# One layer of a hybrid encoder: norm weights as rows, first weights in eight pieces, row sums earlier, last gate projections by quarters

## The chip, the cores and the metric

The kernel runs on one core of a Trainium2 chip. The metric is the device time of one execution in microseconds (us), given as the median of several runs. An engine works through its own queue in order: PE is the matrix engine (PEld its weight loads), DVE the vector engine, ACT the scalar engine, POOL the general engine, SP the engine that issues the DMAs. Each waits on semaphores for what another has made.

## The reference

x has 2048 rows of 1024 columns (f32). The layer normalises each row, multiplies by one input matrix of 1024 x 3344 columns, and splits the result between two head groups.

```
h = rms_norm(x, norm_w)
proj = h @ w_in      # dn_q, dn_k, dn_v, dn_z, beta, decay | sw_q, sw_k, sw_v, sw_z
dn = gated_deltanet_bidir(...)          # 4 heads of 128: conv of 5 taps on q, k, v, SiLU, l2 norm,
                                        # gated delta rule in chunks, forward and backward
dn = rms_norm(dn, dn_out_norm_w) * silu(dn_z)
sw = windowed_gqa_with_sinks(...) * silu(sw_z)   # 8 query and 2 kv heads of 64, window 128
out = x + concat(dn, sw) @ w_out
```

Inputs, results and sums are f32.

## The kernel before

The kernel keeps f32 accuracy with the faster f32r matmuls: each operand is split into a rounded part `hi` (ACT, `AF.Copy`) and the rest `lo` (DVE, subtract), and a product is three matmuls, hi x hi, hi x lo, lo x hi.

**Phase A** (`phase_a`) goes through the rows in two halves of 1024; a half is two blocks of 512 rows, and a block four chunks of 128. A block of normalised, transposed rows is a pair of tiles `xhi[b]`, `xlo[b]`; the pool holds two such pairs, so the second half's blocks 2 and 3 take the places of 0 and 1.

- `xprep_rows` (L102) makes block 0: for each chunk it loads 128 rows of x (`xr`, L104 and L115), sums the squares on ACT (L119), makes the factor on POOL (L120, L121), multiplies by factor and norm weights (`nwb`, one DMA that reads the 1024 weights for each of the 128 partitions, L110) on DVE (L122), transposes on PE (L126) and splits (L129, L130).
- `xprep` (L132) makes blocks 1, 2 and 3: it loads the four row chunks (L137), sums the squares (L138), makes the factors (L139, L140), spreads them over a PSUM bank `rb` with PE (L143), loads x transposed (`xt`, L150), scales it on DVE (L153) and splits (L154, L155).
- `load_w` (L159) loads a weight matrix in four pieces of two row groups each (`ws`) and splits them (L165, L166). The split weights have two places, `wh`/`wl`.
- `proj_seq` (L181) projects a chunk of rows for keys, values, queries and the small gates (`pq_kv`, 272 columns, and `pq_q`, 256): 24 matmuls per chunk. `proj_feat` (L171) projects 128 features of a block (`pf_z`, `pf_c`, 512 columns): 24 matmuls.
- `gate_pair` (L192) takes two groups of gate features through both blocks of a half (tanh on ACT L199, multiply on DVE L200), and stores 1024 columns of each (L202). `conv_pair` (L204) does the same for two groups of q, k or v with the convolution on DVE (L224).
- `attend` (L314) does the window attention of a chunk: scores `s` (L326, L327), mask and maximum on DVE (L328), exponential on ACT (L333), division on POOL (L342), transposes on PE (L347), split (L351, L352) and products `po` (L354, L355).

Tiles of 1024 columns (`xr`, `xt`, gate results, convolution tiles) come from one pool, `bp`, with four places in a ring; the banks of `pq`, `pf` and `rb` from one, `pj`, with three.

The main loop (L369 to L401) makes a half's blocks, its keys, values and queries, then attends chunk after chunk, and after each takes one or two of ten entries of a list `fill`: two gate pairs for the attention, six convolution pairs, and the two gate pairs 12 and 14 for the delta net, which come last in a half. `xprep(2)` stands at the head of the second half.

**Phase B** (`phase_b`) takes the four delta-net heads one after another. `pre_front` (L586) makes the chunk matrices, `pre_back` (L665) solves the triangular systems (31 steps on DVE, L681 and L685, then PE), `scan` (L724) carries the state through 16 steps from both ends, and `post` (L783) normalises four chunks and multiplies by the gate: squares on ACT (L790), a power of four columns on POOL (L793), scaling (L795), transposes. The output projection follows (`out_sw`, `out_dn`, L526).

**The order.** `set_order` (L843) plans the order of all five queues by itself. It lists what each instruction needs (data, and for a tile the end of the last use of the tile whose place it takes), gives each a price (`cost`, L971), plans forward and backward several times and fixes the best order by added dependencies. A change of the program can thus move any instruction on its queue.

Of the kernel before, what the change touches and what calls it, by code (L numbers as in the profile page):

```python
# [7 lines left out]
F32 = mybir.dt.float32  # L8
F32R = mybir.dt.float32r
AF = mybir.ActivationFunctionType  # L10
ALU = mybir.AluOpType
# [4 lines left out]
P = 128  # L16
S = 2048
D = 1024
KC = 8
NCH = 16  # L20
HC = 8
WC = 272
# [41 lines left out]
def phase_a(ctx, tc, t, ident, nw, bd, gp, mix_sw, kq_d, v_d, zdn_d, zsw_d, q_pool):  # L64
# [37 lines left out]
    def xprep_rows(b):  # L102
# [7 lines left out]
        dma(nwb, t["nw"].partition_broadcast(P))  # L110
# [21 lines left out]
    def xprep(b):  # L132
        rs = sp.tile([P, 4], F32, tag="rs", name=f"rs{b}")
# [6 lines left out]
        G.tensor_tensor(rs, rs, half_neg[:, :4], ALU.pow)  # L140
        rb = pj.tile([P, 512], F32, tag="pj", name=f"rb{b}")
# [17 lines left out]
    def load_w(src, n, name):  # L159
        hi = wp.tile([P, KC, WC], F32R, tag="whi", name=f"wh_{name}")  # L160
        lo = wp.tile([P, KC, WC], F32R, tag="wlo", name=f"wl_{name}")
        for kk in range(0, KC, 2):
            st = wp.tile([P, 2, WC], F32, tag="wst", name=f"ws_{name}_{kk}")
            dma(st[:, :, :n], src[:, kk : kk + 2])
            A.activation(hi[:, kk : kk + 2, :n], st[:, :, :n], AF.Copy)  # L165
            V.tensor_tensor(  # L166
                lo[:, kk : kk + 2, :n], st[:, :, :n], hi[:, kk : kk + 2, :n].bitcast(F32), ALU.subtract
            )
        return hi, lo
# [22 lines left out]
    def gate_pair(i, half, dsts):  # L192
        w = load_w(t["wt"][i // 2], 2 * P, f"z{i}_{half}")
        os = [bp.tile([P, 1030], F32, tag="big", name=f"zo{i + j}_{half}") for j in range(2)]
        for nb in range(2):
            for j in range(2):
                ps = proj_feat(w, j * P, 2 * half + nb, f"z{i + j}_{half}_{nb}")
                ov = os[j][:, nb * 512 : (nb + 1) * 512]
                A.activation(ov, ps, AF.Tanh, scale=0.5)  # L199
                V.scalar_tensor_tensor(ov, ov, 1.0, ps, ALU.add, ALU.mult)  # L200
        for j in range(2):
            dma(dsts[j][:, half * 1024 : (half + 1) * 1024], os[j][:, :1024])  # L202
# [166 lines left out]
    for half in range(2):  # L369
        c0 = half * HC  # L370
        (xprep if half else xprep_rows)(2 * half)
# [16 lines left out]
        fill = [lambda i=i: gate_pair(16 + i, half, [zsw_d[i], zsw_d[i + 1]]) for i in (0, 2)]  # L388
        fill += [lambda i=i: conv_pair(i, half) for i in (0, 4, 8, 2, 6, 10)]
        fill += [lambda i=i: gate_pair(12 + i, half, zdn_d[i : i + 2]) for i in (0, 2)]  # L390
        for c in range(HC):
            cc = c0 + c
            if c == 0:
                kv_chunk(cc)
            if c < HC - 1:
                kv_chunk(cc + 1)
            pend.append((cc, q_chunk(cc)))
            while pend and (pend[0][0] < cc or cc == NCH - 1):
                attend(*pend.pop(0))
            for _ in range(nfill[half][c]):  # L400
                fill.pop(0)()  # L401
    with tc.high_priority(-1000000):
        for f in fill:
            f()
# [92 lines left out]
def phase_b(ctx, tc, t, ident, consts, hp, mix_dn, mix_sw, kq_d, v_d, zdn_d, zsw_d, dp, out):  # L497
# [88 lines left out]
    def pre_front(h):  # L586
# [11 lines left out]
        for n, c4 in enumerate(FRONT):  # L598
# [32 lines left out]
            for d in range(2):  # L631
                V.tensor_tensor(bp[:, d, s4], beta[:, s4, 4 * d + h], ssk[:, s4], ALU.mult)
# [91 lines left out]
    def scan(h, H):  # L724
# [3 lines left out]
        for i in range(NCH):  # L728
# [54 lines left out]
    def post(h, H, c4):  # L783
        oa = H["oacc"][c4]
        s4 = slice(4 * c4, 4 * c4 + 4)
        nm = f"{h}_{c4}"
        so = rp.tile([P, 2, 4], F32, tag="so", name=f"sso{nm}")
        for c in range(4):
            jk = rp.tile([P, P], F32, tag="jko", name=f"jko{nm}_{c}", bufs=3)
            A.activation(jk, oa[:, c], AF.Square, accum_out=so[:, 0, c : c + 1])  # L790
        V.tensor_scalar(so[:, 1], H["ssq"][:, s4], EPS, 128.0 * EPS, ALU.add, ALU.mult)
        V.scalar_tensor_tensor(so[:, 0], so[:, 0], 1.0 / 128, so[:, 1], ALU.mult, ALU.add)
        G.tensor_tensor(so[:, 0], so[:, 0], pw[:, 1, :4], ALU.pow)  # L793
        for c in range(4):
            A.activation(oa[:, c], oa[:, c], AF.Copy, scale=so[:, 0, c : c + 1])  # L795
# [47 lines left out]
def set_order(tc):  # L843
# [127 lines left out]
    def cost(i, eng):  # L971
# [155 lines left out]
def layout(inputs):  # L1127
# [6 lines left out]
    def kt(a):  # L1134
        return np.ascontiguousarray(a.reshape(KC, P, a.shape[1]).transpose(1, 0, 2))
# [24 lines left out]
        "nw": g["norm_w"][0], "nwt": g["norm_w"][0].reshape(KC, P).T, "cw": cw, "wout": kt(g["w_out"][0]),  # L1160
# [23 lines left out]
```

## Time and profile before

| | |
|---|---|
| median of 3 runs | 1381.32 us (1380.93 to 1381.75) |
| profiled execution, its own time | 1378.68 us |
| its span in the profile | 1376.9 us |
| mean granted clock of PE | 0.989 |
| PE busy | 1290.2 us (94%) |
| DVE busy | 951.7 us (69%) |
| ACT busy | 689.5 us (50%) |
| POOL busy | 411.0 us (30%) |
| DMA | 201.26 MB, 146 GB/s |

The profile is of one execution. Its page gives busy times, a strip of 40 slices of about 34 us with the busy share in tenths, and the chain of work that ended last. Views of the trace give busy times in chosen windows (each engine's busy time and, in brackets, its number of instructions, then PE's granted clock, the mean busy share of the 16 DMA engines, and GB/s), the waits ("engine line, waited for engine line: us in total, times, longest us"), and instructions in order of time ("start us, duration us, engine, line, operation, output <- inputs, shapes", in square brackets the idle time before it and what ended it). A view of one tile or line gives min/median/max duration in ns. A DMA is "issued" on SP and "lands" later.

### The profile page before, as it was taken

To read this page: it belongs to the slowest core of one execution; us is meant where nothing else is said; L and a number is where in the kernel's file an instruction comes from. 1 tells how busy PE (TensorE), PEld (TensorE's weight loads), DVE (VectorE), ACT (ScalarE), POOL (GpSimd) and SP (SyncE) were. 2 spreads that over 40 slices of the span, in tenths; PEclk is the share of its full clock that TensorE was granted. 3 is DMA by queue.
4 is the path that set the end of the run, shared out by engine and by line. 5 is a ranking of instruction groups with operands and counts; after the bars stand their busy time and mean duration, and the time that the engine had idled before them with its cause. 6 is when DMAs were issued, how large, how long until landed. Compare 5 with 4: busy or idle time off the path is not lost.

```text
span 1376.9 us, 23076 instructions
## 1 busy us (share of the span) xinstructions
PE 1290.2 (94%) x7546; PEld 1107.4 (80%) x7546; DVE 951.7 (69%) x2374; ACT 689.5 (50%) x2021; POOL 411.0 (30%) x570
## 2 busy tenths in 40 slices
PE   4999999999899999999999799999989979999998
PEld 3998878787799888888778577788978969899776
DVE  3422376864752258999887899668998998977632
ACT  4421242434733344777667976308767575465410
POOL 1230012220410223666777664114234042120000
PEclk9999999999899999999999999999989999999999
DMA  6442332234723443222232767986668274243676
GB/s 217 145 131 68 103 107 92 99 98 141 244 94 110 147 131 118 94 86 82 73 97 81 251 188 214 289 262 175 153 175 217 71 223 99 86 115 93 226 245 209
DMA packets 216951, 201.26 MB, mean 146 GB/s; under 512 B 48000, under 2 KB 169600, under 8 KB 216832
## 3 DMA queue, kind: packets, MB, share of 16 engines
q1 hardware_dynamic: 216832, 199.79, 47.7%
q8 instruction: 60, 0.98, 0.3%
q14 instruction: 59, 0.48, 0.1%
HBM read 134.66 MB, written 65.08 MB: 145 GB/s over the span
## 4 chain that ended last, share of the span: by engine, by line
PE 69%; DVE 15%; DMA 5%; ACT 5%; issue 3%; POOL 2%; SPq 0%; DVEq 0%; ACTq 0%; POOLq 0%
PE pf_c L176 6%; PE pf_c L177 6%; PE pf_c L178 6%; PE pw L717 4%; PE pf_z L176 4%; PE pf_z L177 4%; PE pf_z L178 4%; PE pt L347 2%; PE pq_q L187 2%; PE pq_q L188 2%; PE pq_q L189 2%; DVE acc L224 2%; PE pcd L538 2%; PE pcd L539 2%; PE pcd L540 2%
## 5 line engine op out<-in xcount | busy, mean ns | idle before, releaser
L224 DVE SCALAR_TENSOR_TENSOR acc<-pf_c,cw,acc 128x512 f32<-128x512 f32 (+2 forms) x192 | 138.3, 744 | 32.3 <-ACT acc L220 30.9
L176 PE MATMUL pf_c<-xhi,wh_c 128*128 128x512 f32 x384 | 147.3, 399 | 3.8 <-DVE acc L224 3.7
L177 PE MATMUL pf_c<-xlo,wh_c 128*128 128x512 f32 x384 | 146.9, 398 | 0.0
L178 PE MATMUL pf_c<-xhi,wl_c 128*128 128x512 f32 x384 | 145.0, 397 | 0.0
L342 POOL TENSOR_SCALAR pr<-pr,st 128x384 f32<-128x384 f32 (+1 forms) x128 | 79.6, 639 | 55.1 <-DVE st L340 49.4
L333 ACT ACTIVATE pr<-pr,st 128x384 f32<-128x384 f32 (+1 forms) x128 | 76.2, 597 | 26.0 <-DVE st L332 18.9
L176 PE MATMUL pf_z<-xhi,wh_z 128*128 128x512 f32 x256 | 87.3, 403 | 1.9 <-DVE acc L224 1.0
L176 PEld LDWEIGHTS pf_c<-xhi,wh_c 128*128 128x128 f32 x384 | 72.2, 188 | 20.2 <-DVE acc L224 5.1
L177 PE MATMUL pf_z<-xlo,wh_z 128*128 128x512 f32 x256 | 86.6, 399 | 0.0
L178 PE MATMUL pf_z<-xhi,wl_z 128*128 128x512 f32 x256 | 86.2, 400 | 0.0
L178 PEld LDWEIGHTS pf_c<-xhi,wl_c 128*128 128x128 f32 x384 | 72.1, 188 | 15.2
L177 PEld LDWEIGHTS pf_c<-xlo,wh_c 128*128 128x128 f32 x384 | 72.1, 188 | 14.6
L328 DVE CUSTOM_DVE_ANT_0 pr<-s,mask,sink 128x384 f32<-128x384 f32 (+1 forms) x128 | 72.2, 592 | 8.4 <-PE pt L347 4.6
L696 POOL TENSOR_TENSOR xd<-xc,blk 128x512 f32<-128x512 f32 x32 | 40.6, 1279 | 121.6 <-DMA xc<-x_d 57.4
L347 PE MATMUL pt<-ident,pr 128*128 128x128 f32 x368 | 71.4, 280 | 5.8 <-POOL pr L342 2.8
L717 PE MATMUL pw<-W,bm 128*128 128x128 f32 x512 | 73.6, 277 | 0.4 <-DVE W L722 0.2
L752 ACT ACTIVATE yk<-py,ck 128x128 f32<-128x128 f32 x120 | 43.9, 366 | 56.2 <-PE py L747 55.4
L351 ACT ACTIVATE ph<-pt 128x512 fp32r<-128x512 f32 x92 | 53.5, 594 | 36.4 <-PE pt L347 31.8
L352 DVE TENSOR_TENSOR pl<-pt,ph 128x512 fp32r<-128x512 f32 x92 | 62.1, 682 | 13.6 <-ACT ph L351 13.2
L347 PEld LDWEIGHTS pt<-ident,pr 128*128 128x128 f32 x368 | 48.0, 142 | 24.9 <-POOL pr L342 10.1
L717 PEld LDWEIGHTS pw<-W,bm 128*128 128x128 f32 x512 | 65.1, 192 | 1.4 <-DVE W L722 0.6
L166 DVE TENSOR_TENSOR wl_c<-ws_c,wh_c 128x512 fp32r<-128x512 f32 x48 | 39.0, 820 | 38.4 <-PE pf_z L178 18.6
(244 smaller groups left out, 3800.1 us busy)
## 6 DMA issues: line engine op xcount, KB each, us to landing
kqc<-kq_d SPq DMA_DIRECT2D x120, 128.0 KB, 2.8
ws_c<-wt SPq DMA_DIRECT2D x48, 256.0 KB, 3.6
xr<-x SPq DMA_DIRECT2D x16, 512.0 KB, 5.1
ws_z<-wt SPq DMA_DIRECT2D x32, 256.0 KB, 3.7
kq<-kq_d SPq DMA_DIRECT2D x16, 512.0 KB, 5.0
xrs<-x SPq DMA_DIRECT2D x32, 256.0 KB, 4.1
part<-xrs SPq DMA_DIRECT2D x32, 256.0 KB, 3.7
m_d<-ma SPq DMA_DIRECT2D x32, 256.0 KB, 4.4
```

Source lines behind the costliest of these rows:

```text
L176: T.matmul(ps, hi[:, k, cs], xhi[b][:, k], start=(k == 0), stop=False)
L177: T.matmul(ps, hi[:, k, cs], xlo[b][:, k], start=False, stop=False)
L178: T.matmul(ps, lo[:, k, cs], xhi[b][:, k], start=False, stop=(k == KC - 1))
L224: V.scalar_tensor_tensor(av, ps[:, lo:], cw[:, i, k : k + 1], av, ALU.mult, ALU.add)
L328: V.tensor_tensor_reduce(pr[j][:, :n], ps[:, :n], mask[:, lo * P : hi * P], 1.0, sink[:, hh : hh + 1], ALU.add, ALU.max, accum_out=mx[:, j ...
L333: A.activation(pr[j][:, :n], pr[j][:, :n], AF.Exp, bias=nm[:, j : j + 1], accum_out=den[:, j : j + 1])
L342: G.tensor_scalar(pr[j][:, :n], pr[j][:, :n], den[:, j : j + 1], 1.0, ALU.mult, ALU.mult)
L347: T.transpose(pt[:, j], pr[j][:, (kb - lo) * P : (kb - lo + 1) * P], ident)
L351: A.activation(ph, ptf, AF.Copy)
L352: V.tensor_tensor(pl, ptf, ph.bitcast(F32), ALU.subtract)
L717: T.matmul(pw_[:, c], B[:, c], wt[d][:, c], start=True, stop=True)
L752: A.activation(yk, py, AF.Copy, scale=ck[:, d, c : c + 1])
```

## The change

- The norm weights come from the host as 128 equal rows (`nwr`) and are loaded as a plain matrix; before, the DMA read one row 128 times.
- The first weight matrix (`kv0`) is loaded and split in eight pieces of one row group, into tiles of the attention's `pr` ring (six places).
- `xprep` is cut: `xstat` loads the rows and makes the factors; for blocks 2 and 3 it runs in the first half, after the attention's chunks 1 and 3, and keeps the factors in tiles of their own.
- The gate pairs of the first half's end, 12 and 14, go together: both weight matrices are loaded, block 0 of both is projected, then `xprep(2)` stands in the program, then block 1 of both. A result tile holds 512 columns of two groups and is stored at once.
- The ring `bp` has five places.
- In phase B, `post` takes two groups of four chunks together (one power of eight columns); two multiplications of `pre_front` become one.
- The planner's price of a narrow f32 matmul changes.

```diff
-        bp = ctx.enter_context(tc.tile_pool(reuse_waits="tile", name="bp", bufs=4))
+        bp = ctx.enter_context(tc.tile_pool(reuse_waits="tile", name="bp", bufs=5))
...
-        dma(nwb, t["nw"].partition_broadcast(P))
+        dma(nwb, t["nwr"])
...
-    def xprep(b):
-        rs = sp.tile([P, 4], F32, tag="rs", name=f"rs{b}")
+    rows = {}
+
+    def xstat(b):
+        rs = rows[b] = sp.tile([P, 4], F32, tag="rsb", name=f"rs{b}", bufs=2)
...
+    def xprep(b):
+        if b not in rows:
+            xstat(b)
+        rs = rows[b]
         rb = pj.tile([P, 512], F32, tag="pj", name=f"rb{b}")
...
-        for kk in range(0, KC, 2):
-            st = wp.tile([P, 2, WC], F32, tag="wst", name=f"ws_{name}_{kk}")
-            dma(st[:, :, :n], src[:, kk : kk + 2])
...
+        step = 1 if name == "kv0" else 2
+        for kk in range(0, KC, step):
+            if step == 1:
+                st = sp.tile([P, 3 * P], F32, tag="pr", name=f"ws_{name}_{kk}", bufs=6)[:, :n].unsqueeze(1)
+            else:
+                st = wp.tile([P, 2, WC], F32, tag="wst", name=f"ws_{name}_{kk}")[:, :, :n]
+            dma(st, src[:, kk : kk + step])
...
-    def gate_pair(i, half, dsts):
...
+    def gate_pairs(todo, half, mid=None):
+        ws = [load_w(t["wt"][i // 2], 2 * P, f"z{i}_{half}") for i, _ in todo]
         for nb in range(2):
+            for (i, dst), w in zip(todo, ws):
+                o = bp.tile([P, 1030], F32, tag="big", name=f"zo{i}_{half}_{nb}")[:, :1024].rearrange("p (j s) -> p j s", j=2)
+                for j in range(2):
+                    ps = proj_feat(w, j * P, 2 * half + nb, f"z{i + j}_{half}_{nb}")
+                    A.activation(o[:, j], ps, AF.Tanh, scale=0.5)
+                    V.scalar_tensor_tensor(o[:, j], o[:, j], 1.0, ps, ALU.add, ALU.mult)
+                at = half * 1024 + nb * 512
+                for j in range(2):
+                    dma(dst[j][:, at : at + 512], o[:, j])
+            if mid and nb == 0:
+                mid()
...
-        (xprep if half else xprep_rows)(2 * half)
+        if half == 0:
+            xprep_rows(0)
...
+        if half:
+            fill += [lambda i=i: gate_pairs([(12 + i, zdn_d[i : i + 2])], half) for i in (0, 2)]
+        else:
+            fill += [lambda: gate_pairs([(12 + i, zdn_d[i : i + 2]) for i in (0, 2)], half, lambda: xprep(2)), lambda: None]
...
+            if half == 0 and c in (1, 3):
+                xstat(2 + c // 2)
...
-            for d in range(2):
-                V.tensor_tensor(bp[:, d, s4], beta[:, s4, 4 * d + h], ssk[:, s4], ALU.mult)
+            V.tensor_tensor(
+                bp[:, :, s4], beta[:, s4, h :: 4].rearrange("p c d -> p d c"),
+                ssk[:, s4].unsqueeze(1).to_broadcast([P, 2, 4]), ALU.mult,
+            )
...
-                post(h, H, 1)
-                post(h, H, 2)
-        post(h, H, 0)
-        post(h, H, 3)
+                post(h, H, (1, 2))
+        post(h, H, (0, 3))
...
-            return 2 * max(111, m / 1.2 + 5)
+            return 2 * (max(m, size(ins[1]) if len(ins) > 1 else P, 40) / 1.2 + 5)
```

More of the change, by code (lines that the diff above doesn't have):

```diff
@@ L387, in phase_a @@
             consts = delta_setup(tc, t, ident, bd, gp, ap, bp, pj, q_pool)
[L388 removed]
+        fill = [lambda i=i: gate_pairs([(16 + i, [zsw_d[i], zsw_d[i + 1]])], half) for i in (0, 2)]
         fill += [lambda i=i: conv_pair(i, half) for i in (0, 4, 8, 2, 6, 10)]
[L390 removed]
+        if half:
+            fill += [lambda i=i: gate_pairs([(12 + i, zdn_d[i : i + 2])], half) for i in (0, 2)]
+        else:
+            fill += [lambda: gate_pairs([(12 + i, zdn_d[i : i + 2]) for i in (0, 2)], half, lambda: xprep(2)), lambda: None]
         for c in range(HC):
```

45 lines of the change are left out of this document (20 added, 25 removed).

## The prediction

> **What bounds the kernel now.** The page first, then busy time by stretch, then the waits and the chain at the places where TensorE (PE) falls short.
>
> ```profile
> span 1376.9 us, 23076 instructions
> PE 1290.2 (94%) x7546; PEld 1107.4 (80%) x7546; DVE 951.7 (69%) x2374; ACT 689.5 (50%) x2021; POOL 411.0 (30%) x570
> ...
> PE   4999999999899999999999799999989979999998
> ```
> ```profile
> 60.00:80.00 20.00, 20.00 (x164) 19.78 (x163) 6.37 (x11) 5.13 (x13) 2.02 (x6) 1.00 0.21 64
> 120.00:140.00 20.00, 20.00 (x88) 16.18 (x87) 4.46 (x8) 3.69 (x7) 0.10 (x1) 1.00 0.29 102
> ```
> ```profile
> 0.00:27.20 27.20, 6.96 (x29) 5.81 (x30) 11.76 (x17) 12.03 (x23) 4.98 (x14) 1.00 0.67 216
> 27.20:41.80 14.60, 14.60 (x101) 14.60 (x100) 3.37 (x5) 7.87 (x16) 1.12 (x5) 1.00 0.65 195
> 41.80:66.00 24.20, 22.06 (x177) 21.18 (x176) 13.34 (x20) 9.65 (x20) 8.57 (x21) 1.00 0.45 144
> 180.00:260.00 80.00, 76.32 (x339) 61.58 (x338) 61.57 (x89) 28.69 (x48) 21.98 (x33) 1.00 0.32 105
> 338.40:361.50 23.10, 17.13 (x75) 12.11 (x73) 18.92 (x49) 19.38 (x45) 8.70 (x11) 0.85 0.85 283
> 361.50:376.80 15.30, 13.79 (x97) 13.57 (x98) 11.90 (x26) 10.93 (x24) 4.95 (x8) 0.89 0.68 223
> ```
>
> PE is the bound: the strip shows 9 nearly throughout. The columns after the window are PE, PEld, DVE, ACT and POOL busy, granted clock, DMA share, GB/s. Where PE is really full, 20 us hold 88 matmuls of 512 columns (227 ns each) or 164 of 272 and 256 (122 ns each). By these prices PE falls short in two places that the change touches. **The head**: it is 27.2 us before the first projection, and the 96 matmuls of the first four key/value chunks (96 x 0.122 = 11.7 us) then take 14.6. **The turn between the halves**: the last gate projection ends at 338.4, the second half's first four chunks at 376.8. These 38.4 us hold 96 x 0.122 = 11.7 us of projections and some attention: 14 `po` x 0.227, 20 score matmuls of 384 columns x 0.17, 41 transposes x 0.1, together 10.7. About 16 us are lost there, at a clock of 0.85 and 0.89. The chain that ended last runs through both places:
>
> ```profile
> 15.13 7.19 DMA xr<-x
> 24.70 1.28 DVE xr L122
> ...
> 348.04 2.07 ACT xr L138 x4
> 356.56 1.72 PE rb L143 x8
> 358.30 4.04 DVE xt L153 x6
> ```
>
> In the head the fourth row block of x is issued at 15.13 and lands 7.19 us later. At the turn the row sums (L138), the broadcast (L143) and the scaling (L153) follow each other with PE nearly empty.
>
> **The change part by part.** PE's work is unchanged, so the sum is made of lost time. I also use the order in which the planner puts the changed program on each queue.
>
> *Head.* Rows of before:
>
> ```profile
> 15.13 0.36 SPq L115 DMA_DIRECT2D xr<-x  x1
> 16.26 0.33 SPq L164 DMA_DIRECT2D ws_kv<-wkv  x1
> 27.29 0.57 PE L187 MATMUL pq_kv<-wh_kv,xhi 128*128 128x272 f32 x1
> 27.66 0.43 PE L188 MATMUL pq_kv<-wh_kv,xlo 128*128 128x272 f32 x1
> 32.42 0.29 PE L188 MATMUL pq_kv<-wh_kv,xlo 128*128 128x272 f32 x1
> ```
> ```profile
> DMA to landing us min/median/max: 3.5/5.2/7.2
> ```
> ```profile
> DMA to landing us min/median/max: 4.3/6.5/6.7
> ```
>
> (The landings are those of `xr` and of `ws_kv`.) The fourth `xr` was SP's 24th DMA, behind a buffer of the pool of four. Now the pool has five, and it is SP's 16th. In both programs an issue, from the ninth on, waits for the landing of the one eight before it. Counting issues and landings from the start by these rows I get an issue at about 10.4 instead of 15.1, a landing at 14 to 17.6, and, with the 5.0 us that before needs from its landing (22.3) to PE's first projection (27.3), a first projection at 20 to 23. I take 22. Against that, the last weight piece is now SP's 36th DMA, behind q weights and constants, where it was the 26th at 16.26. I expect its issue near 21.4, its landing at 25.7 to 28.1, and it cast by 27 to 29. Until then PE can do seven eighths of three chunks. From 22 us, 11.7 us of work plus 2.4 us at the slow start end at 36; from 29, a last eighth of three chunks (9) and a fourth chunk (24), 33 x 0.122 = 4 us, end at 33, so the pieces don't bind. The fourth chunk's end moves from 41.8 to 36: **6 us**, bounds 3 and 9. The slow start is in the trace: a 272-column matmul lasts 0.43 at 27.7 and 0.29 at 32.4. It stays, as PE has the same pauses.
>
> The four added issues cost 4 x 0.33 us of SP, counted above.
>
> The norm weights as 128 rows: the same 512 KB in the same 128 pieces of the destination. The trace of before shows no such load apart from the rows of x, which land 3.5 to 7.2 us after issue like everything here; I put its own gain at 0 (bounds -1 and +1); the multiply that needs it now stands ahead of the weight piece on DVE.
>
> *Waits of the first half.* The five buffers also free the next convolution pair from the previous pair's store.
>
> ```profile
> PE pf_c L176 <- DVE acc L224: 3.7, 2, 2.1
> ```
> ```profile
> PE pq_kv L188 <- DVE xlo L155: 1.4, 1, 1.4
> ```
>
> Of the 3.7 us in 180 to 260 and the 1.4 at the second block (near 57 us) I take **2 us**, bounds 0 and 5. The row sums moved into the first half are 8 loads of 512 KB, 8 squares on ACT and two short chains on POOL; at 120 to 140 ACT is busy 3.69 of 20 us, POOL 0.10 and DMA 0.29, which hides them. Without that cover they would cost what they cost at the turn now, 2.07 us and more for four squares.
>
> *The turn.* Removed from the chain: row sums and power (before them `rb` cannot run), and the place of the whole block behind the half's last projection. The scaling (eight of 0.74) now runs under the last quarter, 96 x 0.227 = 21.8 us of PE work. But what follows it doesn't. In the planned ACT queue the first piece of the q weights (`wh_q1_0`) stands ahead of all four `xhi2` casts. Its buffer is that of the second gate pair, whose last matmul is the last of the quarter. ACT is a queue, so `xhi2` waits for the end t0 of that projection all the same. Behind it on DVE stand `xlo2` and, between its third and fourth piece, the release of the last two gate banks, one of which the second key/value chunk needs.
>
> ```profile
> L154 ACT ACTIVATE xhi<-xt x4: 1041/1050/1058, 360.5 to 364.8; 128x1024 fp32r<-128x1024 f32 x4
> L155 DVE TENSOR_TENSOR xlo<-xt,xhi x4: 1217/1218/1219, 362.3 to 367.0; 128x1024 fp32r<-128x1024 f32 x4
> ```
> ```profile
> 338.38 0.58 ACT L199 ACTIVATE zo<-pf_z 128x512 f32<-128x512 f32 x1
> 339.12 0.68 DVE L200 SCALAR_TENSOR_TENSOR zo<-zo,pf_z 128x512 f32<-128x512 f32 x1
> 339.81 0.64 ACT L165 ACTIVATE wh_q<-ws_q 128x512 fp32r<-128x512 f32 x1
> ```
>
> From t0: q weights 0.2 to 0.85, or 0.7 later if their load is late (it leaves only when the third `wl_kv1` piece is done); `xhi2` at 2, 3, 4 and, behind a gate, 5.5; `xlo2` at 3.9, 5.1, 6.3 and 8; the gate bank free at 7. Chunk 2 starts at about 7.2, chunks 1 and 2 end at 10.9, chunks 3 and 4 at 17, with about 2 us of attention between. The other 8.7 us of the attention that before did here are done later: 17 + 8.7 = 25.7. A slow spell like that of the head (4.8 us at half speed) would cost up to 2.4 us; I take half of it, 1.2. Gain 38.4 - 26.9 = **11.5 us**, bounds 7 (the q load 4 us late) and 16 (nothing lost).
>
> ```profile
> PE pq_kv L187 <- ACT xhi L154: 1.4, 1, 1.4
> ```
>
> That is the longest wait of PE at the turn, and still the granted clock fell to 0.85. [...]
>
> *Given back, and small edits.* The 8.7 us of attention move behind the turn with their DVE work: 18.92 us of DVE busy in the stretch less 4.04 of scaling, times 8.7/10.7, at most 12 us.
>
> ```profile
> 400.00:420.00 20.00, 20.00 (x170) 20.00 (x169) 7.90 (x21) 7.55 (x16) 0.63 (x2) 1.00 0.38 119
> 600.00:620.00 20.00, 20.00 (x108) 16.68 (x107) 19.36 (x47) 12.99 (x31) 14.02 (x20) 1.00 0.27 94
> ```
>
> At 400 DVE has 12 us to spare in 20, at 600 almost nothing. The new order starts the fifth chunk's scores 6 us of PE work sooner after the turn, so most of it fills the free stretch: I take a loss of 1.5 us, bounds 0 and 12.
>
> ```profile
> L793 POOL TENSOR_TENSOR sso<-sso,pw x16: 1005/1007/1019, 1018.7 to 1298.4; 128x4 f32<-128x4 f32 x16
> L267 POOL TENSOR_TENSOR rsq<-rsq,half_neg x16: 1626/1647/2233, 100.2 to 820.1; 128x8 f32<-128x8 f32 x16
> ```
>
> In `post` two powers of four columns (2 x 1.0 us) become one of eight (1.65): 0.35 us less on POOL eight times, but the first group waits 0.65 longer; the scaling by `beta` saves 16 small DVE operations. All beside PE work: 0, bounds -2 and +3. The planner's price for narrow fp32 matmuls only touches the order.
>
> *Sum*: 6 + 2 + 11.5 - 1.5 = 18 us. The profiled execution took 1378.68 us (span 1376.9 and 1.8 around it); it would take 1360.7. The median of the three runs, 1381.32, lies 2.6 above it, so a median of about **1363 us**.
>
> **The rivals.** *A, the turn is fully covered*, the block's whole work beside the last quarter: `xhi2` would run under the quarter, since its buffer (the first block's) is free by then. For it: the scaling is done in time. Against: the ACT queue. It gives 16 instead of 11.5 and no slow spell, and with a head at 8 about 1356.
>
> *B, the head gains nothing*: weight pieces landing 7 us after issue through a queue of eight in flight put the last one at 32 us instead of 28, and the four chunks at about 38 to 40, or the DVE work moved behind the turn is paid in full (12). For it: landings of 6.5 for `ws_kv`; DVE at 19.36 of 20. Against: the first five of the eight pieces are among SP's first 28 issues, and PE has work with them till then. It gives 1363 + 4 to 1363 + 10.5, 1367 to 1374; I put it at 1371.
>
> *C, slower: a triangular solve loses its cover.* Every operation has a new place, also where nothing is edited.
>
> ```profile
> L681 DVE TENSOR_TENSOR tm<-L,X x124: 173/360/1268, 879.4 to 1194.4; 128x31 f32<-128x31 f32 x8, 128x60 f32<-128x60 f32 x8, 128x87 f32<-128x87 f32 x8, 128x112 f32<-128x112 f32 x8
> L685 DVE TENSOR_TENSOR X<-X,tm x124: 179/361/1254, 879.7 to 1194.7; 128x31 f32<-128x31 f32 x8, 128x60 f32<-128x60 f32 x8, 128x87 f32<-128x87 f32 x8, 128x112 f32<-128x112 f32 x8
> 1000.00:1020.00 20.00, 14.73 (x82) 12.39 (x82) 19.98 (x67) 10.07 (x50) 4.89 (x5) 0.88 0.48 135
> ```
>
> One head's solve is 31 x 0.72 = 22 us of DVE under the scan before it, where DVE is full (19.98 of 20). From the point where its last step comes after the scan's last step, the next scan waits for it, up to 22 us: 1363 + 22 = 1385. Against: in the planned DVE queue the last steps of the three later solves stand at scan steps 12, 13 and 11 of 16, as before (11, 13, 11).
>
> *D, the change doesn't move the end*: the gain of the first half is there, but the seam to the second phase (740 to 860) is worse by as much: within 0.2% of 1381.
>
> **How the numbers follow.** Forecast 0.50, A 0.15, B 0.22, C 0.08, D 0.05. The forecast's bounds are 6 +- 3, 2 +- 2 and 11.5 +- 4.5; taken together they give 1363 +- 7. The range reaches to A below and over B above: 1353 to 1376, which leaves out C, D and the edges of A and B, some 0.2. A measurement of this kernel tells 0.2% (2.8 us) from no change. Faster by more than that: forecast, A and B, less a little for their edges, 0.86; same 0.05; slower 0.09.
>
> **What would show it.** Head: first `pq_kv` matmul at 20 to 23 us, fourth chunk's end near 36; if it starts later than 25 or pauses for `wl_kv` pieces, B. Turn: `rb2` and the eight scalings before the end of the last gate projection, the four `xhi2` casts after `wh_q1` and after that end, and some 17 us from there to the end of the fourth chunk; casts before it mean A. From 400 on, the same stretches shifted by about 19 us. A wait of `pk` or `py` of a head's first scan step on its solve that before did not have means C. My sum is wrong if PE's busy time grows, or if the stretch 500 to 860 lengthens.

## The result and the profile after

The changed kernel takes 1358.46 us (median of 4 runs, 1354.93 to 1361.17) beside 1381.12 of the kernel before on the same chip: a ratio of 0.9836, 95% interval 0.9811 to 0.9860. The profiled execution took 1359.47 us, with a span of 1357.7. The line numbers of the changed kernel are about nine higher in phase A: `pf_c` is L185 to L187, `pq_kv` L196 to L198, the split of a block L161 and L162.

The page of the changed kernel first, its busy times and strips:

```profile
span 1357.7 us, 23034 instructions
PE 1286.7 (95%) x7546; PEld 1106.8 (82%) x7546; DVE 945.8 (70%) x2346; ACT 689.1 (51%) x2025; POOL 414.3 (31%) x562
...
PE   5999989999999999999999899999979989999998
...
PEclk9999999999999999999999899999999999999999
```

The 7546 matmuls are the same. What changed is the time that PE loses between them. The same view by stretch as in the prediction (length, then PE, PEld, DVE, ACT and POOL busy, clock, DMA share, GB/s), cut at the changed kernel's own marks: first projection, end of the fourth key/value chunk, end of the eighth, then the convolutions, and the turn from the last gate projection to the end of the second half's fourth chunk:

```profile
0.00:23.80 23.80, 7.46 (x32) 6.31 (x33) 12.22 (x20) 13.70 (x27) 4.92 (x14) 1.00 0.75 236
23.80:37.60 13.80, 13.80 (x98) 13.80 (x97) 3.86 (x7) 6.97 (x18) 1.60 (x4) 1.00 1.01 339
37.60:62.60 25.00, 24.95 (x203) 24.52 (x202) 12.02 (x19) 8.93 (x21) 11.42 (x22) 1.00 0.26 82
180.00:260.00 80.00, 75.09 (x338) 60.80 (x337) 62.88 (x117) 39.20 (x78) 26.34 (x49) 0.98 0.41 137
336.50:352.20 15.70, 15.21 (x113) 14.25 (x112) 12.15 (x23) 11.30 (x22) 1.12 (x3) 1.00 0.78 248
```

The turn took 38.4 us before and takes 15.7, at a full clock. The convolutions between 180 and 260 did not get faster: 338 matmuls in 80 us where before had 339.

To compare all kernels I use one measure. **Lost time** of a stretch is its length less PE's matmuls in it, each at the spacing of full stretches (0.227 us for 512 columns, 0.124 and 0.117 for 272 and 256, 0.172 for scores, 0.229 for `po`, 0.085 for the attention's transposes, 0.215 for the 256 columns of `gh` in plain f32, 0.111 for the rest). All kernels have the same 7546 matmuls, so another price would shift all their sums alike. Lost time in us, from the traces:

| stretch | before | changed |
|---|---|---|
| start to the end of the fourth key/value chunk | 26.4 | 22.2 |
| from there to the last q projection of half 1 | 6.1 | 3.1 |
| from there to the last gate projection of half 1 | 8.8 | 12.7 |
| the turn | 16.5 | 1.8 |
| from there to the last q projection of half 2 | 1.6 | 2.4 |
| all that follows | 118.7 | 116.3 |
| sum | 178.0 | 158.6 |

So 17 of the 19.4 us were gained by the last q projection. The head and the turn gained, and 4 us were lost in the first half's convolutions, where nothing was meant to change for the worse.

In the head the fourth row load leaves SP at 9.94 (before 15.13), its scaling on DVE starts at 20.59 (before 24.70), the first projection at 23.82 (before 27.29). The timelines of SP, DVE and PE of the changed kernel (start, duration):

```profile
9.94 0.43 SPq L115 DMA_DIRECT2D xr<-x  x1
...
22.61 0.43 SPq L175 DMA_DIRECT2D ws_kv<-wkv  x1
```
```profile
20.59 1.50 DVE L122 SCALAR_TENSOR_TENSOR xr<-xr,rs,nwb 128x1024 f32<-128x1024 f32 x1
```
```profile
23.82 0.58 PE L196 MATMUL pq_kv<-wh_kv,xhi 128*128 128x272 f32 x1
```

At the turn DVE has scaled all eight pieces by 324.8, under the last quarter. ACT does the block's casts right behind the q weights, whose first piece waits 3.41 us for a gate projection (in brackets):

```profile
319.44 5.36 DVE L160 SCALAR_TENSOR_TENSOR xt<-xt,nw,rb 128x512 f32<-128x512 f32 x8 [4.07 <-PE rb L150]
```
```profile
336.30 0.63 ACT L176 ACTIVATE wh_q<-ws_q 128x512 fp32r<-128x512 f32 x1 [3.41 <-PE pf_z L186]
336.84 2.94 ACT L161 ACTIVATE xhi<-xt 128x1024 fp32r<-128x1024 f32 x3
339.69 0.58 ACT L208 ACTIVATE zo<-pf_z 128x512 f32<-128x512 f32 x1
340.17 1.04 ACT L161 ACTIVATE xhi<-xt 128x1024 fp32r<-128x1024 f32 x1
```

That is the order that was forecast. But PE hardly notices; its only listed wait at the turn:

```profile
PE pq_kv L197 <- DVE xlo L162: 0.3, 1, 0.3
```

In the convolutions PE still waits for the accumulation on DVE, longer than before (4.8 us in 180 to 260, before 3.7). The second row is POOL's: it clears the first columns of a new accumulation tile, and waits for the square of a row tile `xr`, whose place in the ring that tile takes:

```profile
PE pf_c L185 <- DVE acc L236: 4.8, 2, 4.3
```
```profile
233.13 0.10 POOL L226 MEMSET acc<- 128x2 f32 x1 [6.87 <-ACT xr L140]
```

That wait of POOL cost PE little: PE's next waits, at 240 and 241, are of 0.13 and 0.43 us. PE's long wait, 4.35 us, ends at 191.62, and the chain behind it is another. Both tiles of a new pair are cleared at 185.81, right behind POOL's work for the attention (L264 to L279), which keeps POOL busy for 6.8 of the 7.7 us from 178.2 to 185.9; then come ACT and DVE:

```profile
185.15 0.71 POOL L279 TENSOR_TENSOR rsk<-rsk,half_neg 128x2 f32<-128x2 f32 x1
185.81 0.13 POOL L226 MEMSET acc<- 128x2 f32 x2
```
```profile
186.11 1.83 ACT L232 ACTIVATE acc<-pf_c,cw 128x512 f32<-128x512 f32 x3
```
```profile
186.87 6.01 DVE L236 SCALAR_TENSOR_TENSOR acc<-pf_c,cw,acc 128x512 f32<-128x512 f32 x9 [0.24 <-issue]
```

### The profile page after: what moved, and what is told of

It is laid out like the page before. It is cut to its first block, busy times and chain, and to the rows that moved or that the text cites. A ratio compares the mean times of both kernels' runs of the same rounds, so it can differ in the third digit from the quotient of the medians.

```text
span 1357.7 us, 23034 instructions
## 1 busy us (share of the span) xinstructions
PE 1286.7 (95%) x7546; PEld 1106.8 (82%) x7546; DVE 945.8 (70%) x2346; ACT 689.1 (51%) x2025; POOL 414.3 (31%) x562
## 5 line engine op out<-in xcount | busy, mean ns | idle before, releaser
L185 PE MATMUL pf_c<-xhi,wh_c 128*128 128x512 f32 x384 | 150.6, 403 | 5.4 <-DVE acc L236 5.4
L236 DVE SCALAR_TENSOR_TENSOR acc<-pf_c,cw,acc 128x512 f32<-128x512 f32 (+1 forms) x192 | 140.1, 743 | 21.8 <-ACT acc L232 20.2
L186 PE MATMUL pf_c<-xlo,wh_c 128*128 128x512 f32 x384 | 150.3, 402 | 0.0
L187 PE MATMUL pf_c<-xhi,wl_c 128*128 128x512 f32 x384 | 148.3, 399 | 0.0
L354 POOL TENSOR_SCALAR pr<-pr,st 128x384 f32<-128x384 f32 (+1 forms) x128 | 86.3, 691 | 35.6 <-DVE st L352 23.7
L186 PE MATMUL pf_z<-xlo,wh_z 128*128 128x512 f32 x256 | 93.7, 398 | 0.0
L185 PE MATMUL pf_z<-xhi,wh_z 128*128 128x512 f32 x256 | 93.5, 398 | 0.0
L187 PE MATMUL pf_z<-xhi,wl_z 128*128 128x512 f32 x256 | 93.0, 398 | 0.0
L185 PEld LDWEIGHTS pf_c<-xhi,wh_c 128*128 128x128 f32 x384 | 72.7, 189 | 21.0 <-DVE acc L236 5.3
L187 PEld LDWEIGHTS pf_c<-xhi,wl_c 128*128 128x128 f32 x384 | 72.6, 189 | 14.6
L186 PEld LDWEIGHTS pf_c<-xlo,wh_c 128*128 128x128 f32 x384 | 72.7, 190 | 13.9
L716 POOL TENSOR_TENSOR xd<-xc,blk 128x512 f32<-128x512 f32 x32 | 41.3, 1300 | 120.3 <-DMA xc<-x_d 59.7
L177 DVE TENSOR_TENSOR wl_c<-ws_c,wh_c 128x512 fp32r<-128x512 f32 x48 | 36.1, 756 | 38.4 <-ACT wh_c L176 25.7
```

The source lines that it names most:

```text
L185: T.matmul(ps, hi[:, k, cs], xhi[b][:, k], start=(k == 0), stop=False)
L186: T.matmul(ps, hi[:, k, cs], xlo[b][:, k], start=False, stop=False)
L187: T.matmul(ps, lo[:, k, cs], xhi[b][:, k], start=False, stop=(k == KC - 1))
L236: V.scalar_tensor_tensor(av, ps[:, lo:], cw[:, i, k : k + 1], av, ALU.mult, ALU.add)
L354: G.tensor_scalar(pr[j][:, :n], pr[j][:, :n], den[:, j : j + 1], 1.0, ALU.mult, ALU.mult)
```

## The experiments

The profile leaves four explanations for the 17 us: the turn part as a whole, one of its halves, the fifth place in the ring, or the two edits of the head. Twelve kernels tell them apart. Their lost time by stretch, as above ("conv" is the third row, "to q2" the sum up to the last q projection, "rest" all that follows):

| kernel | median us | head | to q1 | conv | turn | to q2 | rest |
|---|---|---|---|---|---|---|---|
| before | 1381.1 | 26.4 | 6.1 | 8.8 | 16.5 | 59.3 | 118.7 |
| changed | 1358.5 | 22.2 | 3.1 | 12.7 | 1.8 | 42.3 | 116.3 |
| e1 without the turn part | 1363.8 | 21.7 | 1.6 | 4.8 | 11.1 | 42.4 | 120.3 |
| e2 without quarters | 1361.8 | 21.4 | 2.1 | 11.0 | 1.4 | 39.4 | 121.6 |
| e3 sums late | 1354.3 | 21.2 | 2.1 | 13.9 | 0.7 | 40.0 | 112.1 |
| e4 squares elsewhere | 1354.5 | 20.2 | 2.1 | 8.9 | 0.1 | 32.9 | 119.3 |
| e5 before + ring of five | 1356.5 | 21.2 | 3.7 | 4.3 | 13.2 | 44.7 | 110.4 |
| e6 without the head's edits | 1362.2 | 21.3 | 4.5 | 13.7 | 1.8 | 44.0 | 119.6 |
| e7 own tile, all blocks | 1363.0 | 22.8 | 14.3 | 5.1 | 2.3 | 45.8 | 117.3 |
| e8 e7 + squares elsewhere | 1364.7 | 23.3 | 12.3 | 4.8 | 0.1 | 42.4 | 122.5 |
| e9 own tile, blocks 2 and 3 | 1350.1 | 19.8 | 5.0 | 4.2 | 2.9 | 33.6 | 112.8 |
| e10 e9 + squares elsewhere | 1358.5 | 20.6 | 3.9 | 4.3 | 0.1 | 31.8 | 126.5 |
| e11 old post, beta, price | 1358.1 | 21.0 | 2.2 | 12.8 | 1.8 | 40.5 | 117.9 |
| e12 before + two edits | 1358.4 | 22.1 | 3.7 | 4.3 | 2.9 | 34.7 | 122.6 |

Medians are of four or five runs each, and the lowest and highest run of one kernel lie 2 to 9 us apart; the 2.8 us that the prediction took as the least change a measurement tells was too small for that. The stretches are of one profiled execution.

**e1, the turn part undone.**

```diff
-            if half == 0 and c in (1, 3):
-                xstat(2 + c // 2)
...
-            fill += [lambda: gate_pairs([(12 + i, ...) for i in (0, 2)], half, lambda: xprep(2)), lambda: None]
+        fill += [lambda i=i: gate_pairs([(12 + i, zdn_d[i : i + 2])], half) for i in (0, 2)]
...
+        else:
+            xprep(2)
```

> The changed kernel (1358) with the whole turn part undone: row sums of block 2 and 3 again inside xprep, gate pairs 12 and 14 one after the other, xprep(2) behind the half's last projection. Ring of five, head and phase B as changed. Lost time means a stretch less its matmuls at the prices of full stretches; at the turn (last gate projection to the end of the fourth key/value chunk) the kernel before loses 16 us and the changed one 2. My theory, that the early row sums and the quarters make the gain at the turn: lost time there 12 to 16 again, total 1370 to 1373. Rival 1, the fifth place of the ring alone lets the block be made early: lost time under 5, total near 1360. Rival 2, the whole gain is a luckier plan: total anywhere within 1353 to 1381 without the turn's lost time following.

It took 1363.82 us (1358.27 to 1364.82), ratio 0.9853 (0.9827 to 0.9879). The window over its turn:

```profile
320.20:351.80 31.60, 26.55 (x165) 22.81 (x164) 27.41 (x76) 29.11 (x71) 15.05 (x25) 0.89 0.78 246
```

The turn loses 11.1 us again, a little under my theory's 12 to 16, at a clock of 0.89. Yet the total went up by 5 us only, and up to the last q projection it lost 42.4 us, as much as the changed kernel. For what the turn part gains at the turn it pays in the convolutions: 4.8 us without it, 12.7 with it. My theory of this point fell, and the total lies below the 1370 to 1373 expected: the turn part is not where the net gain is.

**e2, the quarters alone undone; e3, the early sums alone undone.** e2 has the second and third hunk of e1, e3 the first.

> The changed kernel with the quarters alone undone: pairs 12 and 14 one after the other, xprep(2) behind them; the row sums stay early. Theory (the two parts share the gain at the turn): the last two projections of pair 14 that read block 0 end 10.9 us before the half's end instead of 21.8, and the casts of block 2 come after the half's end, so the turn loses 6 to 8 us instead of 2, total 1362 to 1365. Rival 1, the row sums alone are enough: 2 to 3 us lost, total 1358 to 1360. Rival 2, the quarters do it all: 12 to 16 lost, total 1369 to 1373.

> The changed kernel with the early row sums alone undone: they are made in xprep, for block 2 after the third quarter (first of the two blocks of both pairs); the quarters stay. Theory (two parts share): four loads of 512 KB, four squares of 1.0 us, the power and the spreading take some 12 to 15 us of the last quarter's 21.8, the scaling has the rest; the turn loses 3 to 6 us instead of 2, total 1359 to 1363. If the row sums do it all: 10 to 14 us lost, total 1367 to 1371. If the quarters do it all: 2 lost, total 1358.

e2 took 1361.75 us (1358.49 to 1363.20), e3 1354.32 (1352.99 to 1358.56). In e2 the turn loses 1.4 us, with a longest wait of 0.8:

```profile
PE pq_kv L197 <- DVE xlo L162: 0.8, 1, 0.8
```

So the early sums do the turn alone, as rival 1 had it, though the total is above that rival's 1358 to 1360; the quarters add nothing there. In e3 the turn loses 0.7, but the loss stands ahead of it, where the spreading of the factors waits for the sums. The waits of PE from 270 to 351, and the window before the last quarter, with its low clock:

```profile
PE rb L150 <- POOL rs L142: 2.5, 1, 2.5
PE s L338 <- DVE st L340: 1.8, 1, 1.8
```
```profile
274.50:320.00 45.50, 40.86 (x184) 33.40 (x183) 22.63 (x54) 22.18 (x51) 22.54 (x35) 0.89 0.56 183
```

Conv and turn together are 15.9 us without either part (e1), 12.4 with the early sums (e2), 14.6 with the quarters (e3) and 14.5 with both: each way puts most of the same loss in another place. e3's median is nonetheless 4 us lower than that of the changed kernel, and below the 1359 to 1363 expected, but the intervals of the two ratios overlap (0.9777 to 0.9829 and 0.9811 to 0.9860). In the traces 4.2 of the 6.5 us between them lie in the last column, to which I return.

**e4, the head's squares written elsewhere.** The planner takes the places of a ring by first use; the head's squares use block 1's tile before block 0's, so it believes that block 2 stands in block 1's place.

```diff
-        sq = xhi[b + 1].rearrange("p k s -> p (k s)")[:, :D]
+        sq = k2.rearrange("p a b n -> p (a b n)")[:, :D]
```

> The changed kernel with the squares of the head's rows written to the key tile k2 instead of block 1's xhi, so that the planner takes block 2's tiles to stand in block 0's place (which they do) and plans three of its four ACT casts before the last quarter's projections end and ahead of the q weights. Theory (casts behind the last projection cost what the turn still loses): lost time at the turn falls from 1.9 to under 1 us, total 1356 to 1358. The prediction's own reckoning, in which the casts' late place costs 4.5 to 6 us at the turn: total 1352 to 1354. Rival, the plan elsewhere changes more than the turn: total outside 1353 to 1361.

It took 1354.47 us (1353.03 to 1358.25). The turn loses 0.1 us; in the window from the last gate projection's end to that of the fourth chunk PE is never idle:

```profile
336.10:344.20 8.10, 8.10 (x66) 8.07 (x65) 2.58 (x4) 3.07 (x7) 0.48 (x3) 1.00 0.72 215
```

That is the rival A of the prediction made real. It was worth 1.7 us at the turn, as my theory had it, not the 4.5 to 6 of the prediction's own reckoning. The conv column moved too, to 8.9, and with it the total came out below my 1356 to 1358.

**e5, the kernel before with the ring of five alone.**

```diff
-        bp = ... name="bp", bufs=4))
+        bp = ... name="bp", bufs=5))
```

> The kernel before with one change, five places in the ring of 1024-column tiles instead of four. After the first four runs my theory is that this line carries most of the gain, since the changed kernel without its turn part still took 1363.8: the fourth row load of the head leaves earlier (first projection at 23 to 25 instead of 27.3), lost time from the first projection to the end of the first half's projections 3 to 4 us instead of 8.4, in the first half's convolutions about 4 instead of 8, at the turn 11 to 13 instead of 16: total 1364 to 1369. The prediction's sum (ring: part of the head's 6 and 2 us of waits): total 1373 to 1377. Rival, the pieces and the rows of the head carry the head: first projection near 27, total 1370 to 1373.

It took 1356.47 us (1354.97 to 1357.97), ratio 0.9828 (0.9803 to 0.9854), the same as the whole change. One number in one line gives 14.6 of the 17 us up to the last q projection: 5.2 in the head (first projection at 22.80), 2.4 to the last q projection of half 1, 4.5 in the convolutions, 3.3 at the turn, less 0.8 lost behind it. The total is below the 1364 to 1369 expected, because the last column lost 8.3 us less as well, which nothing in this edit aims at. The convolutions without early sums:

```profile
180.00:260.00 80.00, 80.00 (x347) 65.02 (x346) 59.01 (x80) 23.77 (x35) 1.50 (x13) 1.00 0.28 88
```

PE is full for 80 us, and has no listed wait there.

**e6, the head's edits undone** (broadcast load of one row, four pieces; the ring stays).

```diff
-        dma(nwb, t["nwr"])
+        dma(nwb, t["nw"].partition_broadcast(P))
...
-        step = 1 if name == "kv0" else 2
+        step = 2
```

> The changed kernel (1358) with the head's two edits undone: norm weights broadcast by the DMA from one row, first weights in four pieces. The ring of five stays. Theory, the ring makes the head's gain and these two edits little: first projection at 23 to 25 (changed 23.8, before 27.3), fourth key/value chunk's end at 37 to 39, total 1358 to 1361. The prediction, which took the whole 6 us for the five places and the order of the issues and put the rows at 0 and the pieces as not binding: the same 1358 to 1361. Rival, the pieces carry it: first projection again at 26 to 28, total 1361 to 1363.

It took 1362.18 us (1359.11 to 1364.22), with the first projection at 22.75 us and 21.3 us lost in the head, 0.9 less than in the changed kernel. Neither edit makes the head's gain, as theory and prediction had it. The total is above their 1358 to 1361 and inside the rival's 1361 to 1363, whose late first projection did not come; its interval (0.9839 to 0.9897) overlaps that of the changed kernel. The load of the norm weights itself took 5.5 us from issue to landing before and 4.7 as rows. Of the 5.0 us more in the sum of the row, 3.3 are in the last column.

**e7 and e8, a tile of their own for the early sums.** They keep loads and squares, in halves of 512 columns, but take no place in the ring; e8 has e4's edit as well.

```diff
-            xr = bp.tile([P, 1030], F32, tag="big", name=f"xr{b}_{c}")
...
+            for j in range(2):
+                xr = sp.tile([P, 512], F32, tag="xrs", name=f"xr{b}_{c}_{j}", bufs=1)
...
+                dma(xr, t["x"][r0 : r0 + P, 512 * j : 512 * j + 512])
+                A.activation(xr, xr, AF.Square, accum_out=r2[:, j, c : c + 1])
+        G.tensor_tensor(rs, rs, r2[:, 1], ALU.add)
```

> The changed kernel with the early row sums' rows of x loaded in halves (512 columns) into one tile of their own instead of the ring of five (eight loads of 256 KB and eight squares per block, and one more add of four columns). Theory, the early row loads hold the ring's places and make the convolution pairs wait for them: the lost time between the 150th and the 450th convolution matmul (8.7 us in the changed kernel, 1.4 without early sums) falls to 1.4 to 3, the turn stays at about 2, total 1350 to 1354. Rival 1, it is the loads themselves, or ACT's squares, that delay the convolutions: still 6 to 9 us there, total 1356 to 1360. Rival 2, the turn needs the sums earlier than one tile in turn can give them: turn again above 5.

> Both edits of the two faster runs' kind together: own tile for the early row loads (as in the run named e7_own_tile) and the head's squares written to the key tile, so that block 2's casts are planned under the last quarter (as in e4_sq_else, 1354.5, which lost 5.3 us in the convolution stretch and 0.1 at the turn). Theory: convolution stretch 1.4 to 3, turn under 0.5, total 1347 to 1352, the fastest so far. Rival 1, what is saved in the convolutions is lost again in phase B, whose order moves each time: total 1353 to 1357. Rival 2, loads or squares delay the convolutions wherever they land: 1354 to 1356.

They took 1362.95 us (1360.11 to 1363.98) and 1364.72 (1361.56 to 1369.30): both missed the range expected. The convolutions did what the theory said (lost time from the 150th to the 450th matmul 1.2 us in both, changed 8.7). But block 1's row sums are made by the same function, so in these kernels they too went through one tile, eight loads one after the other, at a place where PE has nothing else. The waits of e7 in 38 to 77, and the window:

```profile
PE rb L153 <- POOL rs L145: 4.2, 1, 4.2
```
```profile
38.20:76.40 38.20, 29.51 (x210) 28.64 (x209) 12.49 (x19) 15.35 (x36) 9.66 (x24) 0.82 0.32 95
```

**e9 and e10, the own tile for blocks 2 and 3 alone**, block 1 back in the ring; e10 again with e4's edit.

```diff
+            if b == 1:
+                xr = bp.tile([P, 1030], F32, tag="big", name=f"xr{b}_{c}")
+                dma(xr[:, :D], t["x"][r0 : r0 + P, :])
+                A.activation(xr[:, :D], xr[:, :D], AF.Square, accum_out=rs[:, c : c + 1])
+                continue
```

> The own tile of e7_own_tile again, but for blocks 2 and 3 alone: in that run block 1, whose row sums are made in the same function, went through the one tile too, eight loads in series, and the second block of the head lost 13.3 us instead of 0.6. Here block 1 uses the ring as in the changed kernel. Theory: second block back at 0.6 to 1.5 us lost, convolution stretch (150th to 450th matmul) at 1.2 to 2 as in e7_own_tile (changed kernel 8.7), turn at 2: total 1349 to 1354. Rival: the convolutions gained in e7_own_tile only because everything ran later: stretch at 5 or more again, total 1356 to 1360.

> As e9_own_late, and the head's squares written to the key tile, so that block 2's casts are planned under the last quarter. Theory: convolution stretch 1.2 to 2 us lost, turn under 0.5, total 1347 to 1352, the fastest so far. Rival: phase B's order takes it back as it moves with each edit (its lost time from the 400th score matmul on was 101 to 109 us in the runs so far): total 1352 to 1358.

e9 took 1350.05 us (1347.32 to 1352.18), ratio 0.9769 (0.9746 to 0.9791): faster than both kernels, its interval below that of the change. The convolutions are full, and the turn keeps its gain (2.9 us):

```profile
180.00:260.00 80.00, 80.00 (x348) 65.03 (x347) 58.54 (x80) 23.77 (x35) 1.50 (x13) 1.00 0.28 86
```

It does not follow that it was the places and not the loads or the squares. The squares of both kernels, the changed one's first (e9's from 60 us on):

```profile
L140 ACT ACTIVATE xr<-xr x8: 1043/1056/1072, 177.3 to 241.0; 128x1024 f32<-128x1024 f32 x8
```
```profile
L147 ACT ACTIVATE xr<-xr x10: 619/632/633, 59.9 to 104.8; 128x512 f32<-128x512 f32 x10
```

In the changed kernel they run between the convolutions' matmuls (134 to 292 us). In e9 all are done by 106 us, and the first of these matmuls starts at 136; in e7, e8, e10 and e12 too the squares end before the convolutions begin. So the own tile let the plan move the early sums out of that stretch altogether, and the attention went with them: between the convolutions the five kernels with early sums through the ring (changed, e2, e4, e6, e11) have 27 to 40 matmuls of scores, transposes of the attention and `po`, and one wait of PE of 3.0 to 4.4 us; the other eight kernels with five places have none of these matmuls there, and no wait. That the early sums through the ring bring the loss is shown, since e1 and e3, without them, have no such wait; whether by the places, the loads, the squares or the attention in POOL's queue, these runs don't tell.

e10 loses least of all up to the last q projection (31.8), with full convolutions too. But it took 1358.46 us (1357.25 to 1359.20), for the rest lost 126.5: its rival was right.

**e11, phase B's edits and the price undone.** `post`, the scaling by `beta` and the price of narrow f32 matmuls are those of the kernel before.

```diff
-                post(h, H, (1, 2))
-        post(h, H, (0, 3))
+                post(h, H, 1)
+                post(h, H, 2)
+        post(h, H, 0)
+        post(h, H, 3)
```

> The changed kernel (1358) with phase B's edits undone: post by single groups of four chunks, beta scaled by two operations, the old price of narrow f32 matmuls. Lost time from the first chunk product of the delta heads to the end is 86.5 us in the kernel before and 90.8 in the changed one. The prediction put the edits at 0, bounds 2 faster and 3 slower: total 1355 to 1360. Theory: the 3 to 4 us that phase B lost are the plan's spread and not the edits, total 1355 to 1361. Rival, the edits cost them: 86 to 87 lost, total 1353 to 1355. Also the plan of phase A may change by the price alone.

It took 1358.05 us (1354.97 to 1363.89), as the changed kernel. The edits are worth nothing that shows.

**e12, the kernel before with two edits**, the ring of five and the early sums in their own tile; the other edits are undone, except that a gate result tile still holds 512 columns of two groups.

> The kernel before with two things alone: the ring of five, and the row sums of blocks 2 and 3 early through a tile of their own (as in e9_own_late). No rows of norm weights, four weight pieces, pairs 12 and 14 one after the other with xprep(2) behind them, old post, beta and price; a gate result tile holds 512 columns of two groups, as changed. Theory: the ring and the early sums carry all of phase A's gain, and quarters, pieces and rows add nothing: lost time up to the second half's last q projection 32 to 38 us (before 59.3, changed 42.3, e9_own_late 33.6), total 1347 to 1357, where the width is the spread of what follows (110 to 126 us in the runs so far). Rival, the quarters are needed once the sums are not in the ring's way: 8 to 12 us at the turn, 43 to 48 up to the q projections, total 1359 to 1366. Rival, the head's edits are needed: first projection after 25.

It took 1358.38 us (five runs, 1356.28 to 1360.29), ratio 0.9837 (0.9819 to 0.9855). Up to the last q projection it loses 34.7 us, within the 32 to 38 expected: two edits do there what e9 does with all of them. The total is 1.4 us above the range, since the rest lost 122.6.

## Why the prediction was right, and where it was not

The time lies 4.5 us below the 1363 and within 1353 to 1376. The sum of 18 us against the 19.4 of the traces is closer than its terms: head and waits came 4.7 us short, the turn and what follows it 6.3 us over, and that these nearly cancel is luck.

- **Head, 6 us forecast, 4.2 measured.** The cause was named rightly: the fifth place, and with it the row load's issue at 9.94 (forecast 10.4). The first projection came at 23.8 instead of 22. The last weight piece was issued at 22.61 (forecast 21.4), and the pieces did not bind. Rows of norm weights and pieces were put at nothing, and e6 shows that.
- **Waits of the first half, 2 us of gain forecast, 0.9 of loss measured.** This step failed, in both directions. The ring alone takes 6.9 us out of these stretches (e5: 8.0 against 14.9), and the change with its early sums loses all of that again (15.8). The sentence that failed is that the idle shares of ACT, POOL and DMA "hide" the eight loads and squares. A share over 20 us does not say what stands in a queue at one moment: of the 8.7 us between the 150th and the 450th matmul, about 6 are the one wait of 4.35 us and the slow matmuls behind it (last section), and just ahead of it POOL was busy with the attention that the plan had put there. The places of the ring are the other candidate, since in the order of the program the four row tiles take four places of five between two convolution pairs; it is argued from the program and not shown. e9 loses only 9.2 us in these stretches, but loads and squares moved away in it too.
- **The turn, 11.5 us forecast, 14.7 measured.** The order was right: scaling under the quarter, casts behind the q weights and the last projection. The term was mis-sized: I reckoned pauses of PE of some 3 us and 1.2 us for a slow clock, and the longest wait was 0.3, with the clock at 1.00. PE took the first two chunks by turns as the pieces came (their copies run back to back at 345.86). The prediction credited the quarters and the early sums together; e2 shows that the sums alone are enough, and e5 that 3.3 of the 14.7 us come with the ring alone.
- **The clock.** At the turn of before the granted clock was 0.85 with no wait of PE over 1.4 us, and in e1 0.89 with a longest wait of 1.7; at the changed kernel's turn it was 1.00 with a longest wait of 0.3. So the 1.2 us was not paid: it was an estimate from the slow matmuls of the head (272 columns, in the trace of before 0.23 us apart until 31.7 and 0.13 from 32.4). What brings the clock down these runs don't show; what the traces have of it stands in the last section.
- **Given back, 1.5 us forecast.** To the last q projection of half 2 it is 0.8, and after that 2.4 us were gained. The runs say that this term cannot be had from the profile of before: the rest lay between 110.4 and 126.5 us in fourteen kernels, also where nothing behind the q projections was edited (110.4 in e5, 122.6 in e12, 118.7 before). Each edit gives all queues a new order, but the order need not be all of it. The mean granted clock was 0.995 in e9's profiled execution and 0.986 in e6's, and executions of one and the same kernel differ with it: e1 took 1358.27 us at a mean granted clock of 0.996, and 1363.61 to 1364.82 at 0.986 and 0.987. So a column of one execution holds some us of chance. Nor does the rest follow the convolutions: kernels with full convolutions (e1, e3, e5, e7 to e10, e12) have a mean of 118.1, the other six 118.9. How these 16 us divide between order and clock stays open.
- **Post and beta, 0 forecast.** e11 agrees.
- **The rivals.** A came true for half: the gain of the turn was near its 16, without the casts under the quarter. B's "paid in full" did not come. C would have put some 22 us into the rest, which lost 2.4 less instead; D would have put 18 there.

So the forecast was right by a sum of four terms, two of them too high and two too low. Of the 17 us up to the q projections, 14.6 come from the ring. The rest of the change moved 9.3 us away from the turn (e1 to changed) and put 7.9 into the convolutions.

## What to carry to other kernels

Ask of every load that is moved under other work which buffer it takes, who else needs that buffer, and what the queues hold there at that moment; a low busy share alone doesn't answer it. When a run is to separate a load from the place that it takes, look in its trace where the load went: in e9 it had left the stretch in question. When a change widens a shared ring and adds users to it, test the wider ring alone: here it took as little time as the whole change. Where a planner orders everything anew, compare kernels stretch by stretch, since the parts far from the edit move by more than most edits are worth.

## What the runs showed of the hardware

Slow matmuls followed a pause of PE. In the changed kernel's convolutions a wait of 4.35 us is followed by matmuls 0.42 us apart, and after some 3 us they are 0.23 apart again (start, duration):

```profile
191.62 0.79 PE L185 MATMUL pf_c<-xhi,wh_c 128*128 128x512 f32 x1 [4.35 <-DVE acc L236]
192.22 0.63 PE L186 MATMUL pf_c<-xlo,wh_c 128*128 128x512 f32 x1
192.64 0.63 PE L187 MATMUL pf_c<-xhi,wl_c 128*128 128x512 f32 x1
...
194.35 0.60 PE L185 MATMUL pf_c<-xhi,wh_c 128*128 128x512 f32 x1
194.78 0.42 PE L186 MATMUL pf_c<-xlo,wh_c 128*128 128x512 f32 x1
195.03 0.39 PE L187 MATMUL pf_c<-xhi,wl_c 128*128 128x512 f32 x1
```

Eight matmuls start between 191.62 and 195.03, where 0.227 apart they would have taken 1.8 us: by this estimate the wait cost 1.6 us more than its length. The trace has the granted clock at half from 191.39 to 194.80, and at 1.00 for 3.4 us on either side.

The clock was at half after shorter pauses too. At the turn of before it is at half from 352.96 to 359.79 and again from 363.20 to 366.62. PE was busy for 2.06 of the 3.96 us from 349.00 to 352.96, with single waits of 0.2 to 1.0 us, and for 0.90 of the 3.41 us from 359.79 to 363.20, with two waits of 1.42, the second until 363.53. These are three falls in two traces: at how much idle time it falls was not shown.

A row load of 512 KB under the convolutions landed 4.8 to 8.1 us after its issue in the changed kernel. e9's loads of 256 KB, one after another and ahead of the convolutions, took 2.8 to 4.8 us:

```profile
DMA to landing us min/median/max: 4.8/6.1/8.1
```
```profile
DMA to landing us min/median/max: 2.8/3.3/4.8
```
